# FFN-down of a decoder layer: 32 of 64 squares in a seven-product form, with the weight sums of eight of them made early and kept in HBM

## The chip, the core and the metric

The kernel runs on one core of a Trainium2 chip. Its time is the device time of one execution in microseconds (us). The engines are named as in the profile: PE (matmuls; PEld is its weight loads), DVE (vector), ACT (scalar), POOL, and SP, whose queue issues the DMAs. Each engine works through its own instructions in a fixed order, which the builder writes out before the run.

## The reference

One decoder layer on 256 tokens of width 2048, in float32: a mixer (pooling heads and RWKV heads), a squared-ReLU feed-forward network (FFN) of width 8192, and a gated embedding. The part that matters here is the FFN:

```python
h2 = rms_norm(x, mlp_norm[i])
x = x + jnp.square(jax.nn.relu(h2 @ w_ffn_up[i])) @ w_ffn_down[i]
```

FFN-up is 256 x 2048 by 2048 x 8192, FFN-down is 256 x 8192 by 8192 x 2048. After it comes the gate (`w_ple_gate`, `w_ple_proj`) and a last norm.

## The kernel before

**Precision.** Every float32 operand is split in two: a high part `wh`, rounded by ACT to the type that PE multiplies (`fp32r`), and a low part `wl`, the rest, which DVE subtracts. A product is three matmuls: high by high, high by low, low by high (`mm3`). So each weight tile costs an ACT copy and a DVE subtraction before PE can use it (`split_w`, recorded at L165 and L166).

**Stages.** `ffn_half` runs twice. It makes one half of the FFN's hidden width (8 steps of `gemm_wide`, matmuls at L1115 and L1119, each step with two calls of `square`, which evacuates a bank and stores the squared activations of one pair of 128-row tiles). Then it runs two sweeps of FFN-down over that half. Sweep `np_` makes the output columns of two 512-wide panels, `n0` and `n1`. The four sweeps are called d00, d01, d10 and d11 here: the first digit is the half, the second `np_`. After d11 comes the projection (`pp`) and the transposes `h3`.

**Squares.** A sweep goes through 16 pairs of 128-row weight tiles. A pair, times two column panels and two token tiles, is a 2 x 2 by 2 x 2 block product, called a square: weight blocks b11, b12 (row tile 1), b21, b22 (row tile 2). A plain square takes 8 block products, which is 24 matmuls of 128 x 512. A square in the seven-product form (Winograd's) takes 7 block products, which is 21 matmuls, but needs four sums of weight blocks (`t1` to `t4`) and four sums of activations. The sums of weights are made by DVE in four 512-wide operations (L1234, L1235, L1239, L1240), then split like the weights: `th` by ACT (L1238, L1242), `tl` by DVE (L1241, L1243). `SEVEN = (2, 4, 7, 9, 11, 13)` are the squares of a sweep that use this form: 6 of 16, so 24 of 64 in all.

**Accumulators.** A sweep holds eight PSUM banks: p2, p3, p4 and d22, which both forms add to, and p1, p5, p6, p7, which only the seven-product form uses. After the last seven-product square, p1, p5, p6 and p7 are combined in tiles `u` (L1285 to L1292) and added to the residual stream `x` by `scaled_residual` (L1306). After square 15 the other four banks are added too, by the same line. The next sweep needs all eight banks again.

**Buffers.** Weights arrive through a ring `raw` of four tiles of 512 KB (three and one extra), and `wh` and `wl` are rings of four as well. A square uses two tiles of each ring. The sums have two tiles of 1024 columns each for `t`, `th` and `tl`. A tile is free again when everything that reads it has run.

**Order.** The builder lists each engine's instructions by going through the program in its own model of time: of those that are ready it takes the one with the best priority. Priority is the place in the program, moved forward by `high_priority`: 20000 places for splits and sums, 30000 for residual additions. The DMAs are listed on SP's queue by the same rule.

Of the kernel before, what the change touches and what calls it, by code (L numbers as in the profile page):

```python
# [9 lines left out]
F32 = mybir.dt.float32  # L10
F32R = mybir.dt.float32r
# [29 lines left out]
def trunk(  # L41
# [19 lines left out]
    nc = tc.nc  # L61
# [223 lines left out]
    def rms_stat(srcs, name):  # L285
        s4 = const.tile([128, 2, 2], F32, tag="s4", bufs=2, name=f"s4_{name}")
        for tt in range(2):
            for hf in range(2):
                junk = fp.tile([128, 1024], F32, tag="t", bufs=2, name=f"junk_{name}{tt}{hf}")
                nc.scalar.activation(  # L290
                    junk, srcs[tt][:, hf * 1024 : (hf + 1) * 1024], AF.Square, accum_out=s4[:, tt, hf : hf + 1]
                )
# [871 lines left out]
    keep_at = ["yd"] * 5 + ["a5", "ys", "th"]  # L1164

    def keep():
# [3 lines left out]
        if where == "a5":  # L1170
            w = a8(5, f"gk{kp}", F32R)
            wh, wl = w[:, 0:1024], w[:, 1024:2048]
        else:
            bufs = {"yd": 10, "ys": 2, "th": 2}[where]
            wh, wl = (fp.tile([128, 1024], F32R, tag=where, bufs=bufs, name=f"gk{kp}{c}") for c in "hl")
# [5 lines left out]
    SEVEN = (2, 4, 7, 9, 11, 13)  # L1181
# [10 lines left out]

    def square_plain(src, pr):

        d = fp.tile([128, 1024], F32R, tag="yd", bufs=10, name=f"yd{pr}")
# [8 lines left out]
    def square_seven(src, pr, q):  # L1204

        if q < 4:
            y = a8((0, 1, 2, 5)[q], f"ys{pr}", F32R)[:, 0:1792]
        else:
            y = fp.tile([128, 1792], F32R, tag="ys", bufs=2, name=f"ys{pr}")
        yh, yl = (y[:, c : c + 896].rearrange("p (f t) -> p f t", t=128) for c in (0, 896))  # L1210
        k1t0, k1t1, k2t0, k2t1 = (src[:, c * 128 : (c + 1) * 128] for c in range(4))
        sf = fp.tile([128, 4, 128], F32, tag="u", bufs=3, name=f"sf{pr}")
# [10 lines left out]
    def weights_seven(ra, rb, name):  # L1223

        b11, b21, b12, b22 = ra[:, 0:512], ra[:, 512:1024], rb[:, 0:512], rb[:, 512:1024]
        t = [fp.tile([128, 1024], F32, tag="t", bufs=2, name=f"t{i}_{name}") for i in range(2)]
        th = [fp.tile([128, 1024], F32R, tag="th", bufs=2, name=f"th{i}_{name}") for i in range(2)]
        tl = [fp.tile([128, 1024], F32R, tag="tl", bufs=2, name=f"tl{i}_{name}") for i in range(2)]
        ha, hb = (ring("wh", F32R, f"w7h{i}_{name}") for i in range(2))
        la, lb = (ring("wl", F32R, f"w7l{i}_{name}") for i in range(2))  # L1230
        with tc.high_priority(20000):
            nc.scalar.activation(ha, ra, AF.Copy)  # L1232
            nc.vector.tensor_tensor(la, ra, ha.bitcast(F32), op=ALU.subtract)
            nc.vector.tensor_tensor(t[0][:, 0:512], b12, b11, op=ALU.subtract)  # L1234
            nc.vector.tensor_tensor(t[0][:, 512:1024], b22, b12, op=ALU.subtract)  # L1235
            nc.scalar.activation(hb[:, 512:1024], b22, AF.Copy)
            nc.vector.tensor_tensor(lb[:, 512:1024], b22, hb[:, 512:1024].bitcast(F32), op=ALU.subtract)
            nc.scalar.activation(th[0], t[0], AF.Copy)  # L1238
            nc.vector.tensor_tensor(t[1][:, 0:512], b22, t[0][:, 0:512], op=ALU.subtract)  # L1239
            nc.vector.tensor_tensor(t[1][:, 512:1024], b21, t[1][:, 0:512], op=ALU.subtract)  # L1240
            nc.vector.tensor_tensor(tl[0], t[0], th[0].bitcast(F32), op=ALU.subtract)  # L1241
            nc.scalar.activation(th[1], t[1], AF.Copy)  # L1242
            nc.vector.tensor_tensor(tl[1], t[1], th[1].bitcast(F32), op=ALU.subtract)  # L1243

        def half(h_, l_, c):
# [3 lines left out]
            "b11": half(ha, la, 0), "b21": half(ha, la, 1), "b22": half(hb, lb, 1),  # L1249
            "t1": half(th[0], tl[0], 0), "t3": half(th[0], tl[0], 1),  # L1250
            "t2": half(th[1], tl[1], 0), "t4": half(th[1], tl[1], 1),
# [56 lines left out]
    def ffn_half(hf):  # L1308
        acts = []
        for i in range(8):  # L1310
# [15 lines left out]
            if f == 1:  # L1326
                inv_ms()
# [163 lines left out]
```

## Time and profile before

| | us |
|---|---|
| three runs before | 1203.24, 1206.65, 1208.37 |
| their median | 1206.65 |
| the profiled execution's own time | 1204.18 |
| its span in the profile | 1202.5 |

The span is what the trace covers; 1.68 us of the profiled execution's time lie outside it. FFN-up takes 391.5 to 572.4 us and 740.5 to 921.5 us of the span; the four sweeps take 572.4 to 656.6, 656.6 to 740.5, 921.5 to 1004.6 and 1004.6 to 1089.0 us. A busy PE in these tables is modelled from pipelined instructions, so the length of a stretch and the count of its matmuls say more than the busy share.

### The profile page before, as it was taken

The numbers are of one execution on the slowest core, as the hardware profiler recorded it, in microseconds if no ns is written. First come the engines' busy times: TensorE is split into PE (matmuls) and PEld (weight loads), VectorE is DVE, ScalarE is ACT, GpSimd is POOL, SyncE is SP. The second block draws the span as 40 slices with busy tenths as digits, with TensorE's granted clock in tenths as the row PEclk, the third lists the DMA queues.
The fourth block names the chain that finished last, engine by engine and source line by source line (L and its number), as shares of the span: only waits on it lengthen the run. The fifth ranks groups of instructions, "written<-read, shape, count | busy, mean of one in ns | idle before, by whom it ended". The sixth has DMA issues, their size and how long they took to land.

```text
span 1202.5 us, 18959 instructions
## 1 busy us (share of the span) xinstructions
PE 1170.1 (97%) x7378; PEld 1001.5 (83%) x7378; DVE 847.7 (70%) x1111; ACT 664.7 (55%) x1198; POOL 19.1 (2%) x77
## 2 busy tenths in 40 slices
PE   7899899999999999999999999999999999999997
PEld 6899898878887888888887888888888888877886
DVE  6785698557655666666879788666667788788753
ACT  5946555557554645555555554555545554568743
POOL 4100000000000000000000000000000000000000
PEclk9999899999999999999999999999999999999999
DMA  7353344445656666565656657556655666666741
GB/s 265 122 169 124 133 128 137 138 139 176 193 179 189 177 191 183 186 191 179 192 189 204 200 186 231 184 188 189 182 190 177 203 198 195 228 202 200 259 152 70
DMA packets 60618, 216.92 MB, mean 180 GB/s; under 512 B 6768, under 2 KB 7536, under 8 KB 60144
## 3 DMA queue, kind: packets, MB, share of 16 engines
q1 hardware_dynamic: 60240, 215.20, 55.8%
q8 instruction: 58, 0.95, 0.3%
q10 hardware_dynamic: 288, 0.51, 0.1%
q14 instruction: 32, 0.26, 0.1%
HBM read 213.59 MB, written 2.10 MB: 179 GB/s over the span
## 4 chain that ended last, share of the span: by engine, by line
PE 76%; DVE 11%; DMA 6%; ACT 4%; issue 2%; DVEq 0%; ACTq 0%
PE u_w L1115 20%; PE u_w L1119 10%; PE d_p L1185 9%; DMA raw_d<-in_w_ffn_down_dram 5%; PE d_w L1185 3%; PE o_b L189 2%; PE o_b L188 2%; PE o_b L187 2%; PE d_d L1185 2%; PE gt_b L188 2%; PE gt_b L187 2%; PE gt_b L189 2%; DVE wl_d L166 1%; PE wag_b L369 1%; PE zp_b L187 1%
## 5 line engine op out<-in xcount | busy, mean ns | idle before, releaser
L1115 PE MATMUL u_w<-h,wh_u 128*128 128x512 f32 x1024 | 362.1, 399 | 0.0
L1119 PE MATMUL u_w<-h,wl_u 128*128 128x256 f32 x1024 | 287.7, 281 | 0.0
L165 ACT ACTIVATE wh_u<-raw_u 128x512 fp32r<-128x512 f32 x256 | 147.7, 624 | 174.5 <-issue 133.3
L166 DVE TENSOR_TENSOR wl_u<-raw_u,wh_u 128x1024 fp32r<-128x1024 f32 x128 | 156.5, 1224 | 122.2 <-ACT wh_u L165 122.2
L1115 PEld LDWEIGHTS u_w<-h,wh_u 128*128 128x128 f32 x1024 | 192.5, 188 | 48.0
L1119 PEld LDWEIGHTS u_w<-h,wl_u 128*128 128x128 f32 x1024 | 193.4, 189 | 0.0
L1185 PE MATMUL d_p<-wh_d,yd 128*128 128x512 f32 x480 | 154.6, 390 | 0.6 <-DVE x L1306 0.5
L165 ACT ACTIVATE wh_d<-raw_d 128x512 fp32r<-128x512 f32 x160 | 89.1, 620 | 36.0 <-issue 16.7
L1185 PEld LDWEIGHTS d_p<-wh_d,yd 128*128 128x128 f32 x480 | 90.1, 188 | 20.0 <-ACT wh_d L165 1.3
L166 DVE TENSOR_TENSOR wl_d<-raw_d,wh_d 128x1024 fp32r<-128x1024 f32 x80 | 95.5, 1220 | 13.5 <-ACT wh_d L165 13.1
L1185 PE MATMUL d_p<-wl_d,yd 128*128 128x512 f32 x240 | 93.9, 391 | 0.8 <-DVE wl_d L166 0.8
L166 DVE TENSOR_TENSOR wl_o<-raw_o,wh_o 128x1024 fp32r<-128x1024 f32 x32 | 39.1, 1224 | 34.6 <-ACT wh_o L165 34.6
L1185 PE MATMUL d_d<-wh_d,yd 128*128 128x512 f32 x160 | 55.8, 389 | 0.0
L165 ACT ACTIVATE wh_o<-raw_o 128x512 fp32r<-128x512 f32 x64 | 36.7, 624 | 33.3 <-PE o_b L189 18.2
L1185 PEld LDWEIGHTS d_p<-wl_d,yd 128*128 128x128 f32 x240 | 45.0, 188 | 11.7 <-DVE wl_d L166 2.6
L1238 ACT ACTIVATE th_d<-t_d 128x1024 fp32r<-128x1024 f32 x24 | 25.4, 1059 | 46.0 <-DVE t_d L1235 40.1
L1185 PE MATMUL d_w<-th_d,ys 128*128 128x512 f32 x144 | 48.2, 389 | 0.0
L1242 ACT ACTIVATE th_d<-t_d 128x1024 fp32r<-128x1024 f32 x24 | 25.4, 1059 | 35.1 <-DVE t_d L1240 35.1
L1243 DVE TENSOR_TENSOR tl_d<-t_d,th_d 128x1024 fp32r<-128x1024 f32 x24 | 29.4, 1224 | 19.9 <-ACT th_d L1242 19.6
L1232 ACT ACTIVATE w7h_d<-raw_d 128x1024 fp32r<-128x1024 f32 x24 | 25.4, 1059 | 26.3 <-PE d_p L1185 11.5
L178 PE MATMUL zr_b<-hTh,wh_zr 128*128 128x256 f32 x128 | 38.5, 301 | 1.2 <-ACT wh_zr L165 1.2
L180 PE MATMUL zr_b<-hTh,wl_zr 128*128 128x256 f32 x128 | 37.7, 294 | 2.0 <-DVE wl_zr L166 2.0
(530 smaller groups left out, 2544.0 us busy)
## 6 DMA issues: line engine op xcount, KB each, us to landing
raw_u<-in_w_ffn_up_dram SPq DMA_DIRECT2D x128, 512.0 KB, 3.5
raw_d<-in_w_ffn_down_dram SPq DMA_DIRECT2D x128, 512.0 KB, 4.1
raw_o<-in_w_out_dram SPq DMA_DIRECT2D x32, 512.0 KB, 3.5
raw_gt<-in_w_ple_gate_dram SPq DMA_DIRECT2D x24, 512.0 KB, 4.4
raw_zk<-in_w_in_dram SPq DMA_DIRECT2D x16, 512.0 KB, 4.1
raw_zr<-in_w_in_dram SPq DMA_DIRECT2D x16, 512.0 KB, 3.5
raw_zv<-in_w_in_dram SPq DMA_DIRECT2D x16, 512.0 KB, 3.5
raw_zp<-in_w_in_dram SPq DMA_DIRECT2D x16, 512.0 KB, 3.5
```

What stands on the lines that cost most here:

```text
L165: nc.scalar.activation(wh[:, a * 512 : (a + 1) * 512], raw[:, a * 512 : (a + 1) * 512], AF.Copy)
L166: nc.vector.tensor_tensor(wl, raw, wh.bitcast(F32), op=ALU.subtract)
L178: nc.tensor.matmul(o, w_h, ah, start=first and ct % 2 == 0, stop=False, skip_group_check=True)
L180: nc.tensor.matmul(o, w_l, ah, start=False, stop=last, skip_group_check=True)
L187: nc.tensor.matmul(o, a_h, wh[:, 0:n], start=first, stop=False)
L188: nc.tensor.matmul(o, a_h, wl[:, 0:n], start=False, stop=False)
L189: nc.tensor.matmul(o, a_l, wh[:, 0:n], start=False, stop=last)
L1115: nc.tensor.matmul(bank[:, ct, :].rearrange("p (s t) -> p s t", s=2), wh[:, c], hl, start=k == 0, stop=False, skip_group_check=True,)
L1119: nc.tensor.matmul(bank[:, ct, 0:T], wl[:, c], hl[:, 0, :], start=False, stop=k == 15, skip_group_check=True)
L1185: nc.tensor.matmul(o, l, r, start=first, stop=last, skip_group_check=True)
L1232: nc.scalar.activation(ha, ra, AF.Copy)
L1243: nc.vector.tensor_tensor(tl[1], t[1], th[1].bitcast(F32), op=ALU.subtract)
```

## The change

Eight of 16 squares of each sweep (0, 2, ..., 14) now use the seven-product form, so 32 of 64. For squares 4 and 10 of each sweep the weight sums are made during FFN-up, after steps 1, 2, 4 and 5 of each half (`sums_ahead`): two loads, three DVE operations and a 1 MB store to HBM each. In the sweep they are loaded back into `t`, and of the second weight tile only the half with b21 is loaded. The weights lie in HBM in another order, so that one tile holds b11 and b22 and the other b12 and b21, and the sums are taken with other signs: one operation 1024 wide and two 512 wide. `t`, `th` and `tl` are now one tile of 2048 columns each (one buffer in place of two halves), and `tl` is one operation. The tile `u` of a sweep's end now lies in the same buffer as `t`, and its additions to `x` are two of 1024 columns, at priority 10000. The stored activations trade places: those of seven-product squares lie in eight `ys` buffers, those of plain squares in pairs in the large slots 1, 2, 0 and 5. The kept gate weights (`keep`) move with them.

```diff
-    keep_at = ["yd"] * 5 + ["a5", "ys", "th"]
+    keep_at = ["ys"] * 4 + ["a5", "th", "tl", "t"]
...
-    SEVEN = (2, 4, 7, 9, 11, 13)
+    SEVEN = tuple(range(0, 16, 2))
+    AHEAD = (4, 10)
+    dr = ctx.enter_context(tc.tile_pool(name="dr", bufs=1, space=bass.MemoryType.DRAM))
+    ahead = {}
+
+    def weight_sums(t, ra, rb):
+        b12, b21, b22 = rb[:, 0:512], rb[:, 512:1024], ra[:, 512:1024]
+        nc.vector.tensor_tensor(
+            t[:, 0:2], ra.rearrange("p (c n) -> p c n", c=2), b12.unsqueeze(1).to_broadcast([128, 2, 512]), op=ALU.subtract
+        )
+        yield
+        nc.vector.tensor_tensor(t[:, 2], b22, t[:, 0], op=ALU.add)
+        nc.vector.tensor_tensor(t[:, 3], b21, t[:, 2], op=ALU.subtract)
+        yield
+
+    def sums_ahead(hf, np_, i):
+        ra, rb = (
+            load_raw(w_down[np_, hf * 16 + i, r].rearrange("p a n -> p (a n)"), 1024, f"ta{hf}{np_}_{i}_{r}") for r in range(2)
+        )
+        t = fp.tile([128, 4, 512], F32, tag="t", name=f"ta{hf}{np_}_{i}")
+        with tc.high_priority(20000):
+            for _ in weight_sums(t, ra, rb):
+                pass
+        ahead[hf, np_, i] = dr.tile([128, 4, 512], F32, tag=f"ta{hf}{np_}_{i}", name=f"tad{hf}{np_}_{i}")
+        nc.sync.dma_start(ahead[hf, np_, i], t)
...
+        q = (pr - 1) // 2
+        if q % 2 == 0:
+            plains[:] = [a8((1, 2, 0, 5)[q // 2], f"yd{pr}", F32R)]
+        d = plains[0][:, q % 2 * 1024 : (q % 2 + 1) * 1024]
...
+        y = fp.tile([128, 1792], F32R, tag="ys", bufs=8, name=f"ys{pr}")
...
+    def weights_seven(ra, rb, name, kept_sums=None):
+
+        b21 = rb[:, 512:1024]
+        t, th, tl = (
+            fp.tile([128, 4, 512], dt, tag=tg, name=f"{tg}_{name}") for tg, dt in (("t", F32), ("th", F32R), ("tl", F32R))
...
         with tc.high_priority(20000):
             nc.scalar.activation(ha, ra, AF.Copy)
+            if kept_sums is None:
+                sums = weight_sums(t, ra, rb)
+                next(sums)
+            else:
+                nc.sync.dma_start(t, kept_sums)
+                sums = iter((0,))
             nc.vector.tensor_tensor(la, ra, ha.bitcast(F32), op=ALU.subtract)
-            nc.vector.tensor_tensor(t[0][:, 0:512], b12, b11, op=ALU.subtract)
-            nc.vector.tensor_tensor(t[0][:, 512:1024], b22, b12, op=ALU.subtract)
-            nc.scalar.activation(hb[:, 512:1024], b22, AF.Copy)
-            nc.vector.tensor_tensor(lb[:, 512:1024], b22, hb[:, 512:1024].bitcast(F32), op=ALU.subtract)
-            nc.scalar.activation(th[0], t[0], AF.Copy)
-            nc.vector.tensor_tensor(t[1][:, 0:512], b22, t[0][:, 0:512], op=ALU.subtract)
-            nc.vector.tensor_tensor(t[1][:, 512:1024], b21, t[1][:, 0:512], op=ALU.subtract)
-            nc.vector.tensor_tensor(tl[0], t[0], th[0].bitcast(F32), op=ALU.subtract)
-            nc.scalar.activation(th[1], t[1], AF.Copy)
-            nc.vector.tensor_tensor(tl[1], t[1], th[1].bitcast(F32), op=ALU.subtract)
+            nc.scalar.activation(th[:, 0:2], t[:, 0:2], AF.Copy)
+            next(sums)
+            nc.scalar.activation(hb[:, 0:512], b21, AF.Copy)
+            nc.scalar.activation(th[:, 2:4], t[:, 2:4], AF.Copy)
+            nc.vector.tensor_tensor(lb[:, 0:512], b21, hb[:, 0:512].bitcast(F32), op=ALU.subtract)
+            nc.vector.tensor_tensor(tl, t, th.bitcast(F32), op=ALU.subtract)
...
+            saved = ahead.get((hf, np_, i))
+            ra = load_raw(src[np_, i, 0].rearrange("p a n -> p (a n)"), 1024, f"{name}_0_{i}")
+            if saved is None:
+                rb = load_raw(src[np_, i, 1].rearrange("p a n -> p (a n)"), 1024, f"{name}_1_{i}")
+            else:
+                rb = ring("raw", F32, f"raw_{name}_1_{i}")
+                nc.sync.dma_start(rb[:, 512:1024], src[np_, i, 1, :, 1, :])
             if i in SEVEN:
-                w = weights_seven(ra, rb, f"{name}_{i}")
+                w = weights_seven(ra, rb, f"{name}_{i}", saved)
...
-                    u = [fp.tile([128, 512], F32, tag="u", bufs=3, name=f"u{c}_{name}") for c in range(3)]
-                    nc.scalar.activation(u[0], p1, AF.Copy)
-                    nc.vector.tensor_tensor(u[1], p6, u[0], op=ALU.add)
-                    residual_(n0, 0, u[0])
-                    nc.vector.tensor_tensor(u[2], p7, u[1], op=ALU.add)
-                    nc.vector.tensor_tensor(u[1], p5, u[1], op=ALU.add)
-                    residual_(n1, 0, u[1])
-                    residual_(n0, 1, u[2])
-                    nc.vector.tensor_tensor(u[2], p5, u[2], op=ALU.add)
-                    residual_(n1, 1, u[2])
+                    u = fp.tile([128, 4, 512], F32, tag="t", name=f"u_{name}")
+                    with tc.high_priority(30000):
+                        nc.scalar.activation(u[:, 0], p1, AF.Copy)
+                        nc.vector.tensor_tensor(u[:, 1], p6, u[:, 0], op=ALU.add)
+                        nc.vector.tensor_tensor(u[:, 2], p7, u[:, 1], op=ALU.add)
+                        nc.vector.tensor_tensor(
+                            u[:, 1::2], u[:, 1:3], p5.unsqueeze(1).to_broadcast([128, 2, 512]), op=ALU.subtract
+                        )
+                    for tt in range(2):
+                        residual_(n0, tt, u[:, 2 * tt : 2 * tt + 2].rearrange("p c n -> p (c n)"), 1024)
...
-    def scaled_residual(n, tt, src):
-        xs = xr[tt][:, n * 512 : (n + 1) * 512]
-        with tc.high_priority(30000):
+    def scaled_residual(n, tt, src, wide=512):
+        xs = xr[tt][:, n * 512 : n * 512 + wide]
+        with tc.high_priority(10000 if wide > 512 else 30000):
...
+            if i in (1, 2, 4, 5):
+                q = (1, 2, 4, 5).index(i)
+                sums_ahead(hf, q // 2, AHEAD[q % 2])
...
+    def squares(w):
+        k, n = w.shape
+        b = w.reshape(k // 256, 2, 128, n // 1024, 2, 512).transpose(3, 0, 1, 4, 2, 5)
+        return np.ascontiguousarray(np.stack([b[:, :, [0, 1], [r, 1 - r]] for r in range(2)], axis=2).transpose(0, 1, 2, 4, 3, 5))
```

## What the change does to the time: the prediction

> **What bounds the kernel now.** I read the page's head first, then a table by stage, then the waits of the matmul line of FFN-down.
>
> ```profile
> span 1202.5 us, 18959 instructions
> ...
> PE 1170.1 (97%) x7378; PEld 1001.5 (83%) x7378; DVE 847.7 (70%) x1111; ACT 664.7 (55%) x1198; POOL 19.1 (2%) x77
> ```
>
> PE is busy nearly all the time. The table by stage gives the length of each stretch, then each engine's busy time; the rows are the two halves of FFN-up and the four sweeps.
>
> ```profile
> core 0: us, PE busy (x) PEld busy (x) DVE busy (x) ACT busy (x) POOL busy (x), PEclk, DMA share, GB/s
> 391.50:572.40 180.90, 180.90 (x1028) 156.89 (x1027) 116.83 (x152) 95.12 (x178) 0.00 (x0) 1.00 0.60 186
> 572.40:656.60 84.20, 83.43 (x368) 68.44 (x366) 69.62 (x80) 45.80 (x68) 0.00 (x0) 1.00 0.59 189
> 656.60:740.50 83.90, 83.67 (x366) 68.64 (x367) 69.55 (x79) 43.74 (x65) 0.00 (x0) 1.00 0.62 199
> 740.50:921.50 181.00, 181.00 (x1026) 156.97 (x1025) 118.61 (x151) 92.08 (x170) 0.00 (x0) 1.00 0.62 192
> 921.50:1004.60 83.10, 83.08 (x367) 68.41 (x365) 69.64 (x80) 45.42 (x67) 0.00 (x0) 1.00 0.60 191
> 1004.60:1089.00 84.40, 83.74 (x366) 68.38 (x366) 70.34 (x80) 45.00 (x66) 0.00 (x0) 1.00 0.65 208
> ```
>
> FFN-up never leaves PE idle. In the sweeps DVE is at 83% (69.6 of 84.2), close behind PE. Two pieces of the chain that ended last give the pace of matmuls:
>
> ```profile
> 698.19 4.76 PE d_p L1185 x21
> ...
> 735.23 4.08 PE d_p L1185 x18
> ```
>
> 4.76 / 21 = 4.08 / 18 = 0.2267 us a matmul. A sweep of 6 x 21 + 10 x 24 = 366 matmuls would take 82.97 us; the four take 84.2 + 83.9 + 83.1 + 84.4 = 335.6 us, against 331.9. So 3.7 us of waits lie in the sweeps, and everything else there is matmuls. What ended those waits, from the view of line L1185 (us in all, times; PE and its weight loads counted apart):
>
> ```profile
>   DVE wl_d L166: 3.4, 7
>   ACT wh_d L165: 1.3, 2
>   DVE w7l_d L1233: 0.8, 2
>   DVE x L1306: 0.5, 1
> ```
>
> It is late splits, above all DVE's, and once a residual at the seam between two sweeps.
>
> **Removed.** Eight more squares take 21 matmuls in place of 24: 24 x 0.2267 = **5.4 us** less PE time. With all old waits gone too, 5.4 + 3.7 = 9.1 us is the most that the sweeps can give.
>
> **Inside a sweep.** DVE's pace is read from its timeline at a seam of the kernel before:
>
> ```profile
> 651.56 0.68 DVE L1292 TENSOR_TENSOR u_d<-d_w,u_d 128x512 f32<-128x512 f32 x1
> 652.16 1.40 DVE L1306 SCALAR_TENSOR_TENSOR x<-u_d,s2sq,x 128x512 f32<-128x512 f32 x2
> 653.48 2.35 DVE L166 TENSOR_TENSOR wl_d<-raw_d,wh_d 128x1024 fp32r<-128x1024 f32 x2
> 655.75 2.06 DVE L1306 SCALAR_TENSOR_TENSOR x<-d_p,s2sq,x 128x512 f32<-128x512 f32 x3
> 657.73 1.21 DVE L166 TENSOR_TENSOR wl_d<-raw_d,wh_d 128x1024 fp32r<-128x1024 f32 x1
> ```
>
> From start to start: 0.60 us for 512 columns, 2.27 / 2 = 1.13 for 1024, 1.98 / 3 = 0.66 for a residual of 512. No row has 2048 columns or a repeated operand. Another 512 columns cost 0.53, so I take 2.2 for 2048 and 1.2 for a residual of 1024; the bounds are 1.8 (three of 512) and 2.27 (two of 1024). An operation with a repeated operand I take at the 1.13 of its width; it may cost up to twice that, 1.1 more, in a pair as at the seam. A new seven-product square costs DVE 1.13 (`la`) + 2.33 (sums: 1.13 + 0.60 + 0.60) + 0.60 (`lb`) + 2.2 (`tl`) = 6.3 us, before 3 x 1.13 + 5 x 0.60 = 6.4. With the plain square's 2.27 a pair of squares takes 8.5 us of DVE, against 45 x 0.2267 = 10.2 of PE; with kept sums 6.2. So pairs are covered with 1.7 us to spare.
>
> The single `th` and `tl` add a wait: they are free only when the last matmul of the seven-product square before is done. Count from that square's start. ACT's and DVE's times for the sums:
>
> ```profile
> L1238 ACT ACTIVATE th_d<-t_d 128x1024 fp32r<-128x1024 f32 x24 | 25.4, 1059 | 46.0 <-DVE t_d L1235 40.1 <-DVE t_d L1234 5.8
> ...
> L1236 ACT ACTIVATE w7h_d<-raw_d 128x512 fp32r<-128x512 f32 x24 | 14.9, 619 | 5.3 <-DMA raw_d<-in_w_ffn_down_dram 5.0 <-PE d_p L1185 0.3
> ```
>
> Free at 4.76; two `th` 2.1, `hb` 0.6, `tl` 2.2: ready at 9.7. The next such square starts at 10.2 and needs `tl` after 10 matmuls, at 12.5. 2.8 us of slack: I cost it at nothing. Behind the waiting ACT copy stand the splits of the next plain square, needed only at 15.
>
> Kept sums replace 2.33 us of DVE by a load of 1 MB, issued on SP's queue when `t` is free:
>
> ```profile
> raw_d<-in_w_ffn_down_dram SPq DMA_DIRECT2D x128, 512.0 KB, 4.1
> ...
> x<-in_x_dram SPq DMA_DIRECT2D x2, 1024.0 KB, 5.9
> ...
> 15.00:17.00 2.00, 2.00 (x10) 1.56 (x9) 1.64 (x3) 1.10 (x2) 1.85 (x4) 1.00 1.03 410
> ```
>
> `t` is free when `tl` is done, at 9.7 - 10.2 = -0.5; with 5.9 us it lands at 5.4, 0.6 after `th` is free: slack left 2.2. The raw loads behind it on SP's queue wait for no longer than `t` does. A sweep moves 16 x 1 MB + 2 x 0.75 MB, 18.4 million bytes in 81.6 us: 225 GB/s, where 189 to 208 flow now and 410 have been seen. By the Trainium skill (DMA: Bandwidth & Descriptors, Anatomy of one DMA), whose fit is for another issue path, a transfer takes 2.0 us plus its bytes over 436 GB/s. By that estimate 1 MB takes 4.4 us, 1.5 under the row, and the slack would be whole.
>
> **FFN-up.** Each half gains 4 x 2.33 = 9 us of DVE, eight loads and four stores of 1 MB (8.4 million bytes in all, 46 GB/s over 181 us), and two more seven-product activations, whose extra operations are 128 or 256 columns wide. DVE goes from 117 to some 130 of 181 us. PE takes 180.9 / 64 = 2.83 us a weight tile and the rings hold four: 8.5 us of cover for a disturbance of 2.3. Nothing; if the cover failed, 2.3 us each, 19 in all.
>
> **The seam** (d00 to d01, d10 to d11) is what costs. The last seven-product square is now 14, so one plain square, not two, lies behind it, and the next sweep begins with a seven-product square whose `t` waits for `u`, the same buffer. Count from square 14's start. PE: 14 ends at 4.76, 15 at 10.20; nine matmuls of the next square 0 (p1, p2, p3) need no sums and end at 12.24. DVE, from p6 at 4.08: `u` 0.60 + 0.60 + 1.13; four residuals of square 15, 2.64; two wide ones, 2.4; sums 2.33; `tl` 2.2. That is 11.9, so `tl` is ready at 16.0 at the earliest. With the two splits of square 1, 2.27, it is 18.3.
>
> Whether PE stands still from 12.24 depends on its list. This piece of its timeline, at the end of the first w_out panel, is the evidence:
>
> ```profile
> 321.55 0.39 PE L188 MATMUL o_b<-wl_o,mp 128*128 128x512 f32 x1
> 321.92 0.33 PE L1136 MATMUL h2t<-ident,x 128*128 128x128 f32 x1
> 322.01 0.48 PE L189 MATMUL o_b<-wh_o,mp 128*128 128x512 f32 x1
> 322.32 0.40 PE L187 MATMUL o_b<-wh_o,mp 128*128 128x512 f32 x1
> ...
> 322.79 0.49 PE L1136 MATMUL h2t<-ident,x 128*128 128x128 f32 x3
> ```
>
> In the program all transposes of a panel (`h2t`) stand ahead of the next panel's matmuls. PE runs them mixed: the builder lets ready matmuls pass those that wait. So square 1's matmuls to p2, p3 and d22, 18 of them, will pass square 0's sums and cover until 12.24 + 4.08 = 16.3. They need DVE's 2.27 of splits, so `tl` is at 18.3; with 0.3 for handing over I take **2.3 us of wait at each seam, 4.6 in all**. Bounds: 0 (more of square 2 passes) and 7.1 each (rival B).
>
> At d01's end FFN-up follows and needs neither `t` nor all banks; after d11 the projection's matmuls cover the late additions. Nothing there. Of the old 3.7 us I let half go, 1.8: the regular alternation keeps 1.7 us of slack a pair, and the first matmuls go to p1, whose bank is free early. The sum: -5.4 + 4.6 - 1.8 = **-2.6 us**.
>
> **Rivals.** *A, no seam wait:* the builder fills the seam and the old waits go: -9.1 us. For it: the passing above. Against: DVE has 14 us of work there and PE 12. *B, slower, PE stands at the seam:* its list keeps program order, because the builder's own time sees the sums as ready. The wide residuals have lower priority than splits, so `tl` falls at 18.3 + 1.06 (an uncovered `th`) = 19.4 at worst: 3.8 to 7.1 us a seam, I take 6: -5.4 - 1.8 + 12 = +4.8. It decides from (5.4 + 1.8) / 2 = 3.6 us a seam. A wait so long has a second price, which the end of the kernel shows (length, PE busy, granted clock, DMA):
>
> ```profile
> 1194.00:1196.00 2.00, 0.22 (x2) 1.00 0.00 0
> 1196.00:1198.00 2.00, 0.00 (x0) 1.00 0.00 0
> 1198.00:1200.00 2.00, 0.00 (x0) 0.55 1.00 363
> ```
>
> After some 4 us without matmuls the clock is halved. No row shows for how long; between nothing and a pair at half pace (5 us a seam) I take 1.5, which makes +7.8. The Trainium skill (TensorE: Matmul & The Clock Gate, Part 1) says the same: an idle window of about 3.4 us halves the clock, and a busy one brings it back. By that estimate 1.7 us is lost a seam. *C, the single buffers bind after all:* 0.5 us in each of 28 pairs, +14 - 2.6 = +11. Against: 2.8 us of slack. *D, the kept sums land late:* raw tiles took
>
> ```profile
> DMA to landing us min/median/max: 3.4/4.1/6.2
> ```
>
> so 1 MB may take 5.9 x 6.2 / 4.1 = 8.9 us, 0.8 over the slack: 8 x 0.8 - 2.6 = +4.
>
> **The numbers.** The profiled execution took 1204.18 us, the median is 2.47 higher. Forecast: 1204.18 - 2.6 + 2.47 = **1204 us**, chance 0.50, its own range 1199 to 1209. A: 1197.5, 0.21. B: 1214.5, 0.15. C: 1218, 0.07. D: 1210.5, 0.07. This kernel's measurement tells about 0.5%, 6 us, from no change. Faster than 1200.6: A and a small part of the forecast, 0.26. Slower than 1212.7: most of B, C and a part of D, 0.22. Within: 0.52. The range is 1196 to 1214.
>
> **What would show it.** 24 fewer matmuls in the sweeps; d00 and d10 near 81.6 to 82.5 us, d01 and d11 near 84; at the start of d01 matmuls of square 1 before those of square 0's sums, then a wait released by `tl`; FFN-up still 181 us. Wrong if the first matmul on `th` comes straight after p3 with a long wait (B) or none (A), if `th` waits for PE in every pair and PE for it (C), or if `th` waits for the load of `t` (D).

## The result, and the profile after

The changed kernel took 1219.88 us (median of four runs, 1216.36 to 1222.1), the kernel before 1207.21 us beside it (four runs, 1203.24 to 1208.37). The ratio is 1.0108 with a 95% interval of 1.0072 to 1.0144: **slower by about 1.1%**, some 13 us. The forecast was 1204, no change, with a range up to 1214. The time lies outside the range, on the slow side. The nearest of the forecast's numbers is rival C's 1218; the profile shows that C's mechanism is not the reason, so that nearness is chance.

The profiled execution took 1218.36 us, 1.76 of them outside its span. The head of its page:

```profile
span 1216.6 us, 19002 instructions
...
PE 1175.5 (97%) x7354; PEld 1002.9 (82%) x7354; DVE 877.9 (72%) x1107; ACT 678.2 (56%) x1206; POOL 19.1 (2%) x77
```

There are 24 matmuls fewer (7354 against 7378), as the change says, and yet PE is "busy" 5.4 us longer. PE's busy time counts a matmul at half clock for its whole length (0.63 us below, against 0.39 at full clock), so a rise with fewer matmuls is a first hint of the clock. The table by stage has the same columns as before the change (length, busy time of each engine, granted clock, share of the DMA engines, GB/s); the rows are FFN-up, d00, d01, FFN-up, d10, d11:

```profile
core 0: us, PE busy (x) PEld busy (x) DVE busy (x) ACT busy (x) POOL busy (x), PEclk, DMA share, GB/s
397.20:579.00 181.80, 181.80 (x1033) 157.88 (x1034) 132.12 (x179) 99.05 (x185) 0.00 (x0) 1.00 0.69 230
579.00:661.60 82.60, 82.36 (x362) 67.29 (x361) 66.96 (x65) 45.72 (x65) 0.00 (x0) 1.00 0.62 214
661.60:751.40 89.80, 84.89 (x362) 68.21 (x361) 72.47 (x67) 47.85 (x68) 0.00 (x0) 0.98 0.63 217
751.40:932.30 180.90, 180.90 (x1026) 156.89 (x1025) 133.53 (x177) 94.56 (x175) 0.00 (x0) 1.00 0.70 231
932.30:1015.70 83.40, 82.47 (x363) 67.21 (x362) 67.14 (x65) 45.83 (x65) 0.00 (x0) 1.00 0.62 212
1015.70:1103.40 87.70, 83.66 (x362) 66.86 (x361) 71.32 (x67) 48.40 (x69) 0.00 (x0) 1.00 0.67 232
```

FFN-up is as long as it was: from its first matmul to d00's first it takes 181.8 us in both profiles (the row of before shows 180.9 only because that stretch was begun 0.8 us late). d00 (82.6) is 1.6 us shorter than before, d10 0.3 longer. The loss is in d01 and d11, the sweeps that begin with a seam: 89.8 and 87.7 where 83.9 and 84.4 stood (85.0, when d11 is counted up to the next matmul, as in the table of the experiments). A sweep of 360 matmuls of 0.2267 us would take 81.6.

The next fence is PE's timeline at the beginning of d01 (start, length, engine and line, operation; in brackets the idle time before it and what ended it):

```profile
663.51 0.39 PE L1208 MATMUL d_p<-w7h_d,ys 128*128 128x512 f32 x1
663.74 0.62 PE L1208 MATMUL d_p<-wh_d,yd 128*128 128x512 f32 x2
666.44 0.50 PE L1208 MATMUL d_w<-th_d,ys 128*128 128x512 f32 x1 [2.08 <-ACT th_d L1265]
666.78 0.40 PE L1208 MATMUL d_p<-wl_d,yd 128*128 128x512 f32 x1
667.02 0.63 PE L1208 MATMUL d_p<-wh_d,yd 128*128 128x512 f32 x2
668.22 0.50 PE L1208 MATMUL d_p<-wl_d,yd 128*128 128x512 f32 x1 [0.57 <-DVE wl_d L166]
```

The name of the second operand tells the form: `ys` is a seven-product square, here 0, `yd` a plain one, here 1. Square 0's matmuls without sums are followed by **two** matmuls of square 1, and then the list has a matmul on `th`, for which PE stands 2.08 us. After that its list goes on with square 1. DVE's timeline of the same stretch shows why `th` is late:

```profile
654.57 1.22 DVE L1264 TENSOR_TENSOR w7l_d<-raw_d,w7h_d 128x1024 fp32r<-128x1024 f32 x1
655.71 0.69 DVE L1269 TENSOR_TENSOR w7l_d<-raw_d,w7h_d 128x512 fp32r<-128x512 f32 x1
656.34 0.69 DVE L1319 TENSOR_TENSOR u_d<-d_w,u_d 128x512 f32<-128x512 f32 x1
...
657.79 1.22 DVE L1321 TENSOR_TENSOR u_d<-u_d,d_w 128x1024 f32<-128x1024 f32 x1
659.05 2.48 DVE L1339 SCALAR_TENSOR_TENSOR x<-u_d,s2sq,x 128x1024 f32<-128x1024 f32 x2
661.45 2.06 DVE L1339 SCALAR_TENSOR_TENSOR x<-d_p,s2sq,x 128x512 f32<-128x512 f32 x3
663.42 0.74 DVE L1339 SCALAR_TENSOR_TENSOR x<-d_d,s2sq,x 128x512 f32<-128x512 f32 x1
664.08 1.22 DVE L1187 TENSOR_TENSOR t_d<-raw_d,raw_d 128x1024 f32<-128x1024 f32 x1
665.21 1.22 DVE L166 TENSOR_TENSOR wl_d<-raw_d,wh_d 128x1024 fp32r<-128x1024 f32 x1
666.35 0.69 DVE L1191 TENSOR_TENSOR t_d<-raw_d,t_d 128x512 f32<-128x512 f32 x1
666.95 1.22 DVE L166 TENSOR_TENSOR wl_d<-raw_d,wh_d 128x1024 fp32r<-128x1024 f32 x1
668.09 0.69 DVE L1192 TENSOR_TENSOR t_d<-raw_d,t_d 128x512 f32<-128x512 f32 x1
669.90 2.29 DVE L1270 TENSOR_TENSOR tl_d<-t_d,th_d 128x2048 fp32r<-128x2048 f32 x1 [1.12 <-ACT th_d L1268]
```

DVE works without a pause from 654.57 to 668.78, and all of the sums' chain (L1187, `th`, L1191, L1192, `th`, L1270) stands behind all of `u` and the six residuals. `tl` is ready at 672.19. DVE is then behind for two pairs more: PE waits another 0.8 and 0.7 us for `tl` in them. The waits of PE in d01 and in d11 by the view of waits (total, times, longest):

```profile
PE d_w L1208 <- ACT th_d L1265: 2.1, 1, 2.1
PE d_w L1208 <- DVE tl_d L1270: 1.4, 2, 0.8
PE d_p L1208 <- DVE wl_d L166: 1.4, 2, 0.8
...
PE d_w L1208 <- ACT th_d L1265: 2.1, 1, 2.1
PE d_w L1208 <- DVE tl_d L1270: 1.3, 2, 1.1
PE d_p L1208 <- DVE wl_d L166: 0.6, 1, 0.6
```

That is 4.9 and 4.0 us. And the wait has a second price, seen when the table by stretch is taken in pieces of 3.41 us:

```profile
201.01:204.42 3.41, 1.54 (x13) 1.33 (x12) 3.38 (x6) 1.15 (x2) 0.00 (x0) 1.00 0.46 173
204.42:207.83 3.41, 3.37 (x71) 3.31 (x72) 2.74 (x4) 0.59 (x1) 0.00 (x0) 0.50 0.39 114
...
665.22:668.63 3.41, 1.62 (x6) 1.04 (x7) 3.41 (x5) 1.06 (x1) 0.00 (x0) 1.00 0.34 60
668.63:672.04 3.41, 3.41 (x10) 2.64 (x9) 2.29 (x2) 1.50 (x2) 0.00 (x0) 0.50 1.01 382
```

Behind the wait (last two rows) the granted clock is 0.50 for 3.41 us, which loses 1.7. The first rows lie far ahead of the change, in the mixer: there the clock is halved, too, behind a wait of 1.91 us, for three such pieces (10.2 us); in the profile before the same wait (1.89 us) is followed by full clock. It is one reason why this profile reaches FFN-up at 397.2 us and the one before at 390.7 (its first matmul on `u_w`), although the instructions up to there are the same but for a few of ACT's and the order of two of PE's. Whether that belongs to the change had to be tested as well.

### The profile page after: what moved, and what is told of

It is laid out like the page before. It is cut to its first block, busy times and chain, and to the rows that moved or that the text cites. A ratio compares the mean times of both kernels' runs of the same rounds, so it can differ in the third digit from the quotient of the medians.

```text
span 1216.6 us, 19002 instructions
## 1 busy us (share of the span) xinstructions
PE 1175.5 (97%) x7354; PEld 1002.9 (82%) x7354; DVE 877.9 (72%) x1107; ACT 678.2 (56%) x1206; POOL 19.1 (2%) x77
## 4 chain that ended last, share of the span: by engine, by line
PE 75%; DVE 12%; issue 4%; ACT 4%; DMA 4%; DVEq 0%; SPq 0%; ACTq 0%
PE u_w L1115 20%; PE u_w L1119 10%; PE d_p L1208 7%; PE d_w L1208 3%; DMA raw_d<-in_w_ffn_down_dram 2%; DVE wl_d L166 2%; PE o_b L188 2%; PE o_b L189 2%; PE o_b L187 2%; PE gt_b L187 2%; PE gt_b L189 2%; PE gt_b L188 2%; PE d_d L1208 2%; PE wag_b L369 2%; PE zp_b L187 1%
## 5 line engine op out<-in xcount | busy, mean ns | idle before, releaser
L166 DVE TENSOR_TENSOR wl_u<-raw_u,wh_u 128x1024 fp32r<-128x1024 f32 x128 | 156.3, 1224 | 83.0 <-ACT wh_u L165 82.5
L1208 PE MATMUL d_p<-wh_d,yd 128*128 128x512 f32 x384 | 124.7, 392 | 0.0
L1270 DVE TENSOR_TENSOR tl_d<-t_d,th_d 128x2048 fp32r<-128x2048 f32 x32 | 73.4, 2292 | 52.5 <-ACT th_d L1268 52.5
L165 ACT ACTIVATE wh_d<-raw_d 128x512 fp32r<-128x512 f32 x128 | 70.8, 620 | 33.1 <-PE d_d L1208 22.8
L1208 PEld LDWEIGHTS d_p<-wh_d,yd 128*128 128x128 f32 x384 | 72.5, 189 | 15.0
L1208 PE MATMUL d_p<-wl_d,yd 128*128 128x512 f32 x192 | 75.6, 395 | 3.1 <-DVE wl_d L166 3.0
L166 DVE TENSOR_TENSOR wl_d<-raw_d,wh_d 128x1024 fp32r<-128x1024 f32 x64 | 75.7, 1220 | 3.4 <-ACT wh_d L165 3.4
L1208 PE MATMUL d_w<-th_d,ys 128*128 128x512 f32 x192 | 66.3, 394 | 4.3 <-ACT th_d L1265 4.2
L1265 ACT ACTIVATE th_d<-t_d 128x1024 fp32r<-128x1024 f32 x32 | 34.0, 1062 | 61.1 <-DMA t_d<-tad 29.7
L1208 PEld LDWEIGHTS d_w<-th_d,ys 128*128 128x128 f32 x192 | 36.2, 188 | 13.7 <-ACT th_d L1265 5.0
L1208 PE MATMUL d_p<-w7h_d,ys 128*128 128x512 f32 x128 | 44.8, 390 | 0.0
L1208 PE MATMUL d_w<-tl_d,ys 128*128 128x512 f32 x96 | 38.1, 397 | 2.8 <-DVE tl_d L1270 2.8
```

Source lines behind the costliest of these rows:

```text
L165: nc.scalar.activation(wh[:, a * 512 : (a + 1) * 512], raw[:, a * 512 : (a + 1) * 512], AF.Copy)
L166: nc.vector.tensor_tensor(wl, raw, wh.bitcast(F32), op=ALU.subtract)
L1208: nc.tensor.matmul(o, l, r, start=first, stop=last, skip_group_check=True)
L1265: nc.scalar.activation(th[:, 0:2], t[:, 0:2], AF.Copy)
L1270: nc.vector.tensor_tensor(tl, t, th.bitcast(F32), op=ALU.subtract)
```

## The experiments

The theories. **S**: the seam is the cost; DVE is asked there for more than PE's work can cover. **U**: it is the shared buffer; `t` of square 0 waits for `u`, so a buffer of its own for `u` would mend it. **L**: the changed program falls into more half-clock stretches ahead of FFN-up. **K** (R in one of the expectations): such stretches come at random in any of these programs. All runs below were timed beside the kernel before. The table has the stages of each profile in us, from the first matmul of one to the first matmul of the next ("ahead": of FFN-up; "rest": from d11's end to the end of the span), and the mean granted clock of all timed runs.

| run | ahead | d00 | d01 | d10 | d11 | rest | clock, mean of n runs | median us | ratio to before, interval |
|---|---|---|---|---|---|---|---|---|---|
| before | 390.7 | 84.2 | 83.9 | 83.2 | 85.0 | 112.7 | 0.9915 (59) | 1207.21 (4) | |
| e0_before_again | 392.8 | 84.4 | 84.4 | 83.2 | 84.2 | 112.9 | 0.9912 (10) | 1206.21 | 1.0006, 0.9986 to 1.0026 |
| after | 397.2 | 82.7 | 89.8 | 83.4 | 87.7 | 113.3 | 0.9855 (4) | 1219.88 | 1.0108, 1.0072 to 1.0144 |
| e4_changed_again | 397.4 | 83.3 | 90.4 | 83.1 | 88.7 | 114.9 | 0.9875 (6) | 1219.41 | 1.0106, 1.0074 to 1.0138 |
| e9_changed_third | 392.9 | 82.9 | 91.1 | 83.7 | 87.2 | 115.0 | 0.9873 (6) | 1217.68 | 1.0093, 1.0059 to 1.0128 |
| e1_u_own_buffer | 390.5 | 82.4 | 89.5 | 83.5 | 88.7 | 118.7 | 0.9850 (4) | 1222.67 | 1.0129, 1.0076 to 1.0182 |
| e2_sums_in_sweep | 393.3 | 84.1 | 94.5 | 84.0 | 92.1 | 115.5 | 0.9865 (4) | 1227.51 | 1.0166, 1.0133 to 1.0198 |
| e3_plain_first | 391.2 | 84.6 | 85.4 | 85.1 | 82.4 | 112.1 | 0.9907 (10) | 1207.92 | 1.0007, 0.9982 to 1.0032 |
| e5_early_u | 391.4 | 83.9 | 82.6 | 84.5 | 82.4 | 115.6 | 0.9921 (10) | 1204.22 | 0.9991, 0.9970 to 1.0012 |
| e6_no_wide_residual | 390.3 | 82.8 | 86.2 | 83.2 | 83.7 | 113.2 | 0.9913 (10) | 1207.00 | 1.0015, 0.9994 to 1.0036 |
| e7_early_u_alone | 392.8 | 83.2 | 89.5 | 83.3 | 87.8 | 112.6 | 0.9897 (6) | 1215.73 | 1.0075, 1.0046 to 1.0104 |
| e8_swap_seam_only | 395.7 | 83.8 | 84.3 | 84.7 | 86.6 | 111.9 | 0.9918 (12) | 1207.63 | 1.0016, 0.9998 to 1.0034 |

FFN-up is 181.7 to 181.8 and 180.9 to 181.0 us in every profile.

**The kernel before once more, unchanged.** It says how much two runs of one program differ.

> The kernel before once more, for its clock. Of the 14.1 us between the two profiled spans, 6.6 lie ahead of FFN-up, where both programs are the same. Theory K (stretches of half clock come at random): single runs of this kernel show granted clocks from 0.985 to 0.994 and times that follow them, about 1 us per 0.001. Rival L (they belong to the changed program): all runs here stay at 0.993 or more, and the changed kernel and its variants at 0.984 to 0.987.

1206.21 us, ratio 1.0006. Its profile needs 2.1 us more ahead of FFN-up than the other profile of the same program, with half-clock stretches in other places. Its ten runs have clocks from 0.989 to 0.994, where L asked for 0.993 or more in all, so the first half of L's claim fails here.

**A buffer of its own for `u`.**

```diff
-                    u = fp.tile([128, 4, 512], F32, tag="t", name=f"u_{name}")
+                    u = fp.tile([128, 4, 512], F32, tag="u", name=f"u_{name}")
```

(The small tiles that had the tag `u` were moved into one tile of 2048 columns.)

> The changed kernel with the tile u in a buffer of its own, so that the sums of the next sweep's square 0 do not wait for the wide residuals. Theory U (the shared buffer makes the seam's wait): the two second sweeps fall from 89.8 and 87.7 us to under 84 each, the whole by 8 to 11 us. Rival S (DVE has more work at the seam than PE's cover, whatever the buffer): the sums come earlier, but the residuals' 2.4 us only move behind them; 2 to 4 us for both seams, most of the wait stays.

1222.67 us, no gain. d01 and d11 took 89.5 and 88.7, as in the changed kernel (89.8 to 91.1 and 87.2 to 88.7). **Theory U falls**; S's own 2 to 4 us for both seams did not come either. The sweeps are what counts here, not the whole: the edit also moved the projection's operand into the buffer that `u` holds to the end, and PE waits 4.3 us for it behind d11 (118.7 us follow d11). Its timelines: PE's wait first, then what DVE had in the 8 us before it (between the lines shown lie two splits of 2.35 us together and the first sum of square 2, and between the last two its second):

```profile
662.11 0.79 PE L1208 MATMUL d_p<-w7h_d,ys 128*128 128x512 f32 x1 [3.97 <-DVE x L1339]
```

```profile
653.90 2.29 DVE L1270 TENSOR_TENSOR tl_d<-t_d,th_d 128x2048 fp32r<-128x2048 f32 x1
...
659.51 1.28 DVE L1339 SCALAR_TENSOR_TENSOR x<-u_d,s2sq,x 128x1024 f32<-128x1024 f32 x1
...
661.30 0.75 DVE L1339 SCALAR_TENSOR_TENSOR x<-d_p,s2sq,x 128x512 f32<-128x512 f32 x1
```

Here the sums come first (`tl` of square 0 is done at 656.19, 1.6 us after d01 begins; in the changed kernel it is 10.6 us after) and the residuals that free the banks come late. The same DVE work stands at the same seam in another order, and PE waits for its other end.

**No sums ahead:** all weight sums are made in the sweep that uses them.

```diff
-            if i in (1, 2, 4, 5):
+            if False and i in (1, 2, 4, 5):
```

> No sums are made ahead: all 32 squares sum in the sweep, and the eight loads and stores of 1 MB are gone. If kept sums do what the DVE budget says (a pair with sums takes 8.5 of 10.2 us of DVE), they are not needed inside a sweep: the same time within 3 us, FFN-up 1 us shorter. If the sweeps need them to catch up behind the seam: d01 and d11 longer by 2 to 6 us. If their loads stand in the way (the wait of th for the load of t, 29.7 us in the page): shorter by 1 to 4 us.

1227.51 us, about 8 more than the changed kernel. d01 and d11 are 94.5 and 92.1 us, d00 and d10 only 84.1 and 84.0. So the kept sums do help, and mostly there, behind a seam, where DVE has arrears to work off. This is the second of the three outcomes that were named beforehand.

**A plain square first.** The second sweep of each half visits the squares in the order 1, 0, 3, 2, ..., 15, 14. Nothing else is changed, and all that is computed is the same.

```diff
-        for i in range(npair):
+        turn = [i ^ np_ for i in range(npair)]
+        for i in turn:
```

(The last seven-product square and the last plain one are taken from `turn`, and a residual is issued when its bank has had its last product.)

> The second sweep of each half goes through the squares as 1, 0, 3, 2, ..., 15, 14, so that two plain squares lie between square 14 of the first sweep and the next seven-product square; u still shares its buffer with t. Rival S: the plain square covers 5.4 us more, the seam's wait falls from some 8 and 6 us to 1 to 2 each, the whole is 8 to 12 us shorter than the changed kernel. Theory U: the same direction, since the chain is the same but the need comes 5.4 us later; the two are told apart by the run with u in its own buffer. If the seam is not the cause, nothing changes.

1207.92 us, ratio 1.0007: **some 12 us are gone**, and with them the difference to the kernel before. The waits of PE in d01, and the sweeps d01 and d11 by stage:

```profile
PE d_p L1208 <- DVE x L1342: 1.1, 1, 1.1
PE d_w L1208 <- DVE tl_d L1270: 0.2, 1, 0.2
```

```profile
657.50:742.90 85.40, 82.29 (x360) 67.29 (x360) 71.03 (x68) 48.03 (x68) 0.00 (x0) 1.00 0.62 213
...
1009.00:1091.40 82.40, 82.14 (x360) 67.43 (x361) 69.28 (x65) 46.75 (x66) 0.00 (x0) 1.00 0.68 231
```

DVE's busy time hardly changes (71.0 against 72.5 in d01). What changed is that DVE has a plain square's time more between the residuals of one sweep and the first sums of the next. The waits behind the seam sum up to 1.3 us where 4.9 stood, and no stretch of half clock lies in the four sweeps. This is theory S. The edit has a price of its own: a seven-product square now stands last in d01, and FFN-up's first matmul, just behind the window of the waits, waits 2.9 us for `u` to free its bank.

```profile
742.95 0.50 PE L1115 MATMUL u_w<-h,wh_u 128*128 128x512 f32 x1 [2.93 <-DVE u_d L1322]
```

The four sweeps together take 337.5 us, 7.2 less than the changed kernel's mean and still 1.2 more than before.

**The changed kernel again**, for theory L.

> The changed kernel once more, for a second trace of it. Theory R (stretches of half clock ahead of FFN-up come at random, those behind the seams follow the seams' waits): the part ahead of FFN-up takes 390 to 394 us, as in most traces of any variant, not 397.2; the sweeps again take 171 to 174 us a half, FFN-up 181, with one or two stretches of half clock just behind a seam or in the projection; the whole is again 10 to 16 us over the kernel before. Rival L (the change lowers the clock everywhere): the part ahead of FFN-up is again at 396 or more.

1219.41 us. Ahead of FFN-up it took 397.4 us, with the same pattern of half-clock stretches as the first profile: what L expected. But two of its runs took 1213.21 and 1214.61 us at a clock of 0.992 and 0.991, so the pattern isn't always there. Undecided; the third repeat below goes on with it.

**Early `u`, with the swap.** In the last seven-product square of a sweep the products come in the order p1, p6, p7, p5, p2, p3, p4, so that `u` can begin while nine matmuls are still to come; with the swap of e3.

```diff
+                if fin:
+                    products = tuple(products[q] for q in (0, 5, 4, 3, 1, 2, 6))
```

> Plain square first in the second sweeps, as in the run before, and in each sweep's last seven-product square the products p1, p6, p7, p5 go first, so that u can be made 2 us earlier. If what is left of that variant's waits (2.9 us of FFN-up for u's first addition, 1.0 us at the seam for p2's residual) is DVE being asked late: both fall to under 0.5 us, the whole is 2 to 5 us below that variant, 1203 to 1206. If DVE is simply full there, the waits move and the time stays within 1.5 us of 1207.9.

1204.22 us, ratio 0.9991, the best of all, yet not to be told from the kernel before. The four sweeps take 333.4 us against 336.3 before, 2.9 less of the 5.4 that the matmuls save. The 2.9 us in front of FFN-up are gone; the wait for a residual at each seam is still 0.8, where under 0.5 was expected. But with a seven-product square last in d11 the end is worse: PE waits 2.2 us for ACT in the gate, and 115.6 us follow d11 where 112.7 stood.

**No wide residuals in the first sweeps** (d00 and d10): the additions of `u` to `x` are left out there, which takes 2.4 us from DVE at each seam. That part of the sum is missing in this kernel's output.

```diff
-                    for tt in range(2):
+                    for tt in range(2) if np_ else ():
```

> The changed kernel without the two wide residual additions of the first sweep of each half (u is made but not added to x). It takes 2.4 us of DVE work out of each seam and frees the buffer of t as early. Theory S (DVE is asked for more at the seam than PE covers): the second sweeps get shorter by 2 to 4 us each, the whole by 4 to 8. If the wait comes of something else there (the list's order of the splits, the weights' arrival), under 2 us in all.

1207.00 us: 12 to 13 less than the changed kernel. The row of d01:

```profile
654.80:741.10 86.30, 83.14 (x362) 67.21 (x361) 69.77 (x64) 47.73 (x68) 0.00 (x0) 1.00 0.65 226
```

4.8 us of DVE work give more than twice as much, and more than the 4 to 8 us that S expected. The first wait is now 0.8 us, no stretch of half clock lies in the sweeps or at the end of d11, and d01 and d11 are 3.5 to 5 us shorter each. Some late `tl` and `wl` stay (2.2 us in d01). A seam that is over by little costs much.

**Early `u` without the swap.** The product order of e5 alone.

> The changed kernel with only the products' order in each sweep's last seven-product square changed (p1, p6, p7, p5 first). DVE can begin u 2 us earlier, so by theory S the seam's wait falls by about 2 us each, the whole by 3 to 6 us, and the order of squares is worth the remaining 6 to 9 us. If the builder's lists do not use the earlier start, nothing changes.

1215.73 us. The median is 4 us under the changed kernel's, but its interval of the ratio (1.0046 to 1.0104) overlaps that kernel's. d01 and d11 stay at 89.5 and 87.8, so the seam isn't mended: to have `u`'s products nine matmuls (2 us) earlier isn't enough. The first wait falls only from 2.1 to 1.8 us, not by the 2 that were expected. DVE has no free time there to use: it works without a pause from 645.94 us to the second `th`, and with `u` moved forward the splits and residuals only move behind it, so the sums begin 2.1 us after d01 does, where it was 2.5. What the run gains by its profile lies in the rest, 112.6 against 113.3 to 115.0, and its mean clock is higher (0.9897).

**The swap only where it is needed:** the second sweep visits 1, 0, 3, 2 and then 4, 5, ..., 15, so that a plain square stands last again.

```diff
+        turn = [1, 0, 3, 2, *range(4, npair)] if np_ else range(npair)
```

> The second sweep of each half visits 1, 0, 3, 2 and then 4, 5, 6 to 15 in order, so that only its beginning is swapped; the products of the last seven-product square come in the order p1, p6, p7, p5, p2, p3, p4. Theory S (the seam is the cost, and the swap is needed only until DVE has caught up): d01 and d11 stay at 82.5 to 84 us as with the swap of all pairs, because square 4's sums are kept ones and its neighbour 2 is a square later than its own turn; and with a plain square last, as in the change, the way from the end of d11 to the end of the kernel goes back from 115.6 us (the run with both edits and all pairs swapped) to 112 to 113.5. In all 1200 to 1204 us, ratio 0.995 to 0.999 against before. Rival C (the single th and tl bind when two seven-product squares are neighbours, 2 and 4): th waits for square 2's last matmul, PE stands for 2 to 4 us there in each second sweep: d01 and d11 at 85 to 87, in all 1204 to 1209.

1207.63 us, ratio 1.0016: the hoped-for gain did not come. The rest is 111.9 us, as expected. But d11 took 86.6, for which the view of waits lists 3.1 us:

```profile
PE d_w L1208 <- DVE tl_d L1270: 1.8, 4, 0.9
PE d_p L1208 <- DVE x L1345: 0.8, 1, 0.8
PE d_w L1208 <- ACT th_d L1265: 0.5, 1, 0.5
```

Half a microsecond of `th` in square 4, behind its neighbour 2, and 0.9 of `tl` in square 6: small arrears, a mild form of the rival C that was named for this run, whose 85 to 87 us for d11 and 1204 to 1209 in all fit; d01 (84.3) has 1.1 us of such waits. The time itself also has 395.7 us ahead of FFN-up in it, so the profile alone overstates.

**The changed kernel a third time.**

> The changed kernel as it is, a third time, for the part ahead of FFN-up, whose instructions are those of the kernel before. Theory L (the changed program falls into more half-clock stretches there): again 396 us or more ahead of FFN-up, with stretches near 204 us, and 1218 to 1222 in all. Theory K (such stretches come at random in any of these programs): 390 to 394 us ahead of FFN-up, and a profiled time of 1211 to 1215. The seams under both: d01 89 to 91 us, d11 87 to 89.

1217.68 us; 392.9 us ahead of FFN-up: here theory L misses. K has the stage right, but not the profiled run's time (1217.04 where 1211 to 1215 was expected), since d01 took 91.1 us and half clock came behind both seams and at the end of d11. The same place of the mixer as in the fence above, in this run's own pieces of 3.41 us:

```profile
198.83:202.25 3.42, 1.90 (x16) 1.69 (x15) 3.32 (x7) 1.15 (x2) 0.00 (x0) 1.00 0.44 161
202.25:205.66 3.41, 3.03 (x93) 2.86 (x95) 3.37 (x5) 0.59 (x1) 0.00 (x0) 1.00 0.38 143
```

```profile
202.63 1.20 PE L740 MATMUL gm<-T1G,SC 32*32 32x32 f32 x64 [1.90 <-DVE T1G L716]
```

The same wait, 1.90 us, and full clock. The kernel before has this wait in both of its profiles (first profile, then second):

```profile
202.06 1.20 PE L740 MATMUL gm<-T1G,SC 32*32 32x32 f32 x64 [1.89 <-DVE T1G L716]
201.51 1.20 PE L740 MATMUL gm<-T1G,SC 32*32 32x32 f32 x64 [1.91 <-DVE T1G L716]
```

The difference is where it falls. In all twelve profiles the half-clock stretches of a run start on one grid of 3.413 us (to within 2 ns), and where that grid lies differs from run to run. This was worked out from the traces' clock records and PE's instructions. Of the 43 stretches (those at the kernel's very end left out), 42 followed a piece of the grid in which PE was busy for 0.51 of the time or less. From where the clock's records begin, 10 to 13 us into the span, every piece at full clock with less than 0.44 was followed by half clock. Between 0.44 and 0.51 both happened: ten pieces were followed by half clock and 13 were not. In the changed kernel's first profile the wait emptied one piece to 1.54 of 3.41 us, here it is shared between two (1.90 and 3.03). So the clock ahead of FFN-up is chance, theory K, and the kernel before has it as well: its second profile shows a stretch of 6.8 us behind this wait, its first none. (That stretch is the one of the 43 that doesn't fit: PE counts as busy for 0.65 of the piece before it. The matmuls there are of 32 x 32, and how such ones count is open.)

## Why the prediction was wrong

Point by point, by its own steps:

- **Removed: right.** 24 matmuls fewer.
- **Inside a sweep: right for the sums, not for the length.** In d00 and d10 PE never waits for `th` or `tl`. But they took 82.7 and 83.4 us where "81.6 to 82.5" was expected (82.9 to 83.7 in the other two profiles of the changed kernel). The durations that no row had shown were well taken: `tl` 2.29 us for 2048 columns, and the operation with a repeated operand 1.22 us, no slower than one without. Loaded sums are late for ACT (it stood 29.7 us in all for the DMA of `t`), and PE's waits for `th` lie at the two seams alone: rivals C and D did not come.
- **FFN-up: right.** DVE went to 132 of 181.8 us, 230 GB/s flowed, and the length stayed.
- **Old waits: wrong.** They were to fall by half, -1.8 us. In d00 and d10, the two sweeps without a seam in front, the time over the bare matmuls rose instead, from 1.5 and 1.7 us in the two profiles of before to 2.9, 3.2 and 3.4. More than half of it is one wait for `wl` in square 13. There DVE's list has the first sum of square 14 ahead of square 13's splits, and DVE stands 1.3 to 1.4 us for square 14's weights, in all four sweeps of the first profile. In e2, which has no kept sums, DVE's list has the splits first and PE never waits for `wl` there. So this wait comes with the kept sums; whether by the list's order or by their loads, which stand ahead of the weights on SP's queue, was not tested.
- **The seam: this is the step that failed**, "2.3 us of wait at each seam, 4.6 in all". d01 and d11 took 8.2 and 6.1 us more than their matmuls, and the first wait ended with `th`, not with `tl`. Three things in that working were wrong.
  1. *"Square 1's matmuls to p2, p3 and d22, 18 of them, will pass square 0's sums."* Matmuls did pass, but only two before PE's list has the first matmul on `th`. The list is fixed in the builder's own time; in it the sums were ready earlier. PE then stands for `th` (2.08 us). ACT had all of square 1's `wh` done at 663.35, and DVE freed the last bank at 664.16, so there were matmuls on `wh` that PE could have done meanwhile. This reading comes from the rows alone; a kernel with only PE's order changed wasn't tried.
  2. *"`tl` is at 18.3"* after square 14's start (651.43). It was ready at 672.19, 20.8 after. The tally left out two splits that stand ahead of `u` (L1264 and L1269: `u` began at 656.34, 0.8 us after p6 was done) and the uncovered second `th` (1.12 us), which only rival B had priced. The half microsecond that remains is spread.
  3. The wait was costed once. DVE's `tl` came 4.5 us behind what 18 matmuls would have covered. With only 1.7 us of slack a pair, DVE made PE wait twice more for `tl`, and there was the half clock. Counted from the start of each of PE's matmuls to the next, less 0.2267 us, d01's 8.2 us are 3.2 at the seam itself (`th`, then `wl` of square 1), some 1.6 of half clock, 2.0 for `tl` in the next two pairs and 1.1 for the late `wl` of square 13; 0.3 are spread. (The view of waits shows less, since it counts a wait from the modelled end of the matmul before, 0.39 us after its start.)
- **The end of d11: wrong**, at "Nothing there." The projection's first matmuls waited 2.0 us for a residual, and the stage from d11 to the gate took 15.6, 17.2 and 17.1 us in the three profiles of the changed kernel against 14.2 and 14.3.
- **Rival B named the right place and the two prices**, but its mechanism, plain program order, did not hold: squares 0 and 1 are mixed. Its 1.5 us of half clock a seam is near the 1.7 measured in d01; behind d11's seam the first profile has none, the other two have one stretch each.
- **The clock.** The prediction put the halving at "some 4 us without matmuls". The runs show half of that: one wait of 2 us is enough if it falls into one piece of the grid. The Trainium skill (TensorE: Matmul & The Clock Gate, Part 1) says that the window is 3413 ns long and free-running, with which the grid agrees. It also says that an idle window of about 3.4 us halves the clock; here windows in which PE was busy for 0.44 to 0.47 of the time did so, too, and the measurement decides.

The sum of it, by the means over the profiles (three of the changed kernel, two of the kernel before): the sweeps 344.7 against 336.3 us, so 8.4 more where 2.6 less was forecast. By the forecast's own terms that is 5.4 less for the matmuls, as said; 12.3 more in d01 and d11, where 4.6 was said; and 1.6 more in d00 and d10, where the old waits were to give 1.8 back in all. From d11's end to the gate it is 16.6 against 14.2, so 2.4 more, where nothing was forecast; from there to the end 0.8 less. That is 10.0 us. The mean times lie 12.2 us apart (1218.4 for the 12 runs of the changed kernel's two repeats, 1206.2 for the 59 of the kernel before beside the experiments).

The runs' clock gives another cut: 0.9874 against 0.9915, and in the kernel before a thousandth of clock goes with 0.98 us from run to run, so by this estimate 4 of the 12 us are half clock and 8 are waits. A stretch of 3.41 us costs 0.0014 of a run's mean clock, so the difference is some three stretches; the profiles show one, three and three of them in the second sweeps and at the end of d11. The kernels without long waits at a seam (e3, e5, e6, e8) have the old clock, 0.9907 to 0.9921, though the part ahead of FFN-up is the same in all. The 2.2 us between 10.0 and 12.2 are not placed. Ahead of FFN-up the profiles of the changed kernel have 395.8 us in the mean against 391.8, but there the grid's chance is larger than that (390.3 to 397.4 in kernels that are the same up to there); more profiles would be needed to say that no part of it is systematic.

So the change does bring its 5.4 us of matmuls, and the time over the bare matmuls grows by some 14 us in the sweeps (4.4 to 18.3) and by 2 at the end. With the seam mended by an order of squares (e5) the sweeps keep 2.9 us of the 5.4, and no version was shown to be faster than the kernel before.

## What to carry to other kernels

Budget every engine at the joint of two loops by itself: a mean of 83% for DVE over a sweep said nothing about 14 us of its work in one piece there, and a joint that is over by 2 us costs several times that, in follow-on waits and in clock. Mend such a joint by the order of the work (a step that needs little from the late engine first): that gave 12 us here, where another buffer gave nothing, and work asked of the full engine 2 us earlier left both sweeps as long as they were. An engine's list is written before the run, so count on ready work passing a wait only as far as the builder's own time saw the wait coming.

## What the runs showed of the hardware that was not expected

The clock of TensorE is decided piece by piece on a grid of 3.413 us whose place differs from run to run. A wait of 1.89 to 1.91 us at one and the same matmul (L740) cost nothing more in eight of the twelve profiles (the first of before and e9 among them), and 6.8 or 10.2 us of half clock followed it in four (e0; after, e4 and e8). What counts is how much of a piece the wait empties: 0.45 of busy time in the piece at 201.01 us halved the clock, 0.56 at 198.83 us did not. The line is not sharp, since between 0.44 and 0.51 both happened. In the sweeps and at the end of d11 no piece with more than 0.48 was followed by half clock. So there a wait that leaves PE busy for more than half of any 3.4 us was free of this second price, and a wait of 2 to 3 us paid it by chance, 1.7 us for each piece.
